# The second norm's stage of a diffusion block in written order: four output and four feed-forward tiles by token halves

## The chip, the cores and the metric

The kernel runs on one core of one Trainium2 chip. The metric is the device time of one execution in microseconds. The core's engines work side by side, each through its own queue in order: TensorE (PE, matmuls), VectorE (DVE), ScalarE (ACT), GpSimd (POOL), and SyncE (SP), which only issues transfers between HBM and on-chip memory. They wait for each other by semaphores.

## The reference, cut to what matters

One layer on 512 latent tokens of 1024 channels in float32. The change touches the passage from the mixer's output projection to the feed-forward network:

```python
x = x + g1 * (y_merged @ w_out)                       # output projection, gated residual
h2 = rmsnorm(x, norm2_g) * (1.0 + sc2) + sh2           # second norm, modulated
x = x + g2 * ((silu(h2 @ w1) * (h2 @ w3)) @ w2)        # SwiGLU, D_FF = 2816
return rmsnorm(x, final_g)

def rmsnorm(x, g):
    return x * lax.rsqrt(jnp.mean(x * x, axis=-1, keepdims=True) + EPS) * g
```

`sh1, sc1, g1, sh2, sc2, g2` come from a product of the conditioning vector with `w_ada` (adaLN).

## The kernel before, in words

Activations lie with channels on the 128 partitions and tokens along the free axis: a 1024-channel activation is 8 tiles of 128 x 512. Every float32 factor is split into a high part (rounded to fp32r) and a low remainder, and a product is three matmuls per tile of 128 channels: high weights by high input, high by low, low by high (`mm3`, lines 233 to 235; `gemm` calls it for k = 0 to 7). So one output tile of 128 channels is 24 matmuls into one PSUM bank; `psG` and `psH` hold four banks each.

Weights come as 512 KB tiles: `wsplit` takes a raw buffer `wr` (four of them, shared with the adaLN rows), loads it from SP's queue, lets ACT copy it to the high part `wh` and DVE subtract to the low part `wl` (line 215). There are four buffers of `wh` and four of `wl`; a new weight tile waits until PE has finished with the one four tiles earlier.

The second norm's stage:

- `staged_gemms("wout", ...)` does the output tiles 0 to 4 (KT - LAST = 5 of 8) over all 512 tokens. `out_tile` (lines 1459 to 1463) then adds the gated product to the residual `xr` on DVE, squares the sum on ACT and adds the square to `acc1` on DVE. The sum stays in `x1`, in the buffers named K.
- The last three output tiles go by token halves of 256 (`last_tile`): first all three for tokens 0 to 255, then for 256 to 511.
- `half_sums` sums the squares over the channels by matmuls with ones (lines 1472, 1473). `half_rms` takes mean and root (DVE, then POOL's power of -0.5, line 391) and spreads the root over the partitions with two matmuls (line 393).
- `norm2` makes the normalised input of one half, per channel tile k: `t` on DVE (line 1511: x1 times the scale am2 times the root), the high tile hTh on ACT (line 1512: t plus shift), and the low tile hTl on DVE (line 1513: t plus shift minus hTh).
- The first three feed-forward tiles (`jobs`: w1 tile 0, w3 tile 0, w1 tile 1) also go by halves; all others over 512 tokens in the loop over `f`, which calls `background()` once per f: that runs one step of `ada_later`, a load of 512 KB of w_ada into `wr` and a multiply-and-sum of 128 x 1024 on DVE (line 372) for the gate of the feed-forward network.

What sets the order: the kernel is recorded in program order and a scheduler reorders the instructions of each engine within data dependencies. `tc.high_priority` (in `wsplit`) moves instructions ahead, and `behind()` holds instructions until the matmuls of the last `gemm` are issued.

Of the kernel before, what the change touches and what calls it, by code (L numbers as in the profile page):

```python
# [1 line left out]

# [13 lines left out]
D = 1024  # L16
# [143 lines left out]
def build(nc, tc, I, out, dbg=None):  # L160
# [42 lines left out]

    def dump(name, ap):
        if dbg is not None and name in dbg:
            dma(dbg[name], ap)
# [179 lines left out]
    def rms_bcast(sums, nblk, pbank, p, tag):  # L386
        v = T(PW, [128, 8], F32, "rv", 2)
        for i, c in enumerate(sums if isinstance(sums, list) else [sums]):
            dve.tensor_scalar(v[:, i : i + c.shape[-1]], c, 1.0 / D, EPS, op0=ALU.mult, op1=ALU.add)  # L389
        r = T(PW, [128, 8], F32, "rr", 2)  # L390
        gp.tensor_tensor(r[:, :nblk], v[:, :nblk], negh[:, :nblk], op=ALU.pow)  # L391
        for b in range(nblk):
            pe.matmul(pbank[:, 128 * b : 128 * b + 128], r[:, b : b + 1].broadcast_to([128, 128]), ident, start=True, stop=True)

# [1071 lines left out]
    def half_sums(acc, sq, hf):  # L1466

        cols = []
        for b in range(2):
            sl = slice(256 * hf + 128 * b, 256 * hf + 128 * b + 128)  # L1470
            s_ = bank()[:, 0:1]
            pe.matmul(s_, acc[:, sl], ones[:, 0:1], start=True, stop=False)
            pe.matmul(s_, sq[:, sl], ones[:, 0:1], start=False, stop=True)
            cols.append(s_)
        return cols

    def half_rms(cols):
        rb = bank()
        rms_bcast(cols, 2, rb, PF, "s2")
        return rb  # L1480
# [18 lines left out]
    def last_tile(hf, d):  # L1499
        wh, wl = ws[d - KT + LAST]  # L1500
        ps = bank(psG)
        gemm(ps, wh, wl, [half(t, hf) for t in y[0]], [half(t, hf) for t in y[1]], 256)
        return out_tile(ps, 256, d, g1h, 256 * hf, xr[d], x1[d], acc1)

    def norm2(hf, cols):
        with behind():
            rb = half_rms(cols)
        for k in range(KT):
            t = scr()
            sh = modT[:, 3, k, 0:1]  # L1510
            dve.scalar_tensor_tensor(t[:, :256], half(x1[k], hf), am2[:, k : k + 1], rb[:, :256], op0=ALU.mult, op1=ALU.mult)
            act.activation(half(h2[0][k], hf), t[:, :256], AF.Identity, bias=sh)
            dve.scalar_tensor_tensor(half(h2[1][k], hf), t[:, :256], sh, half(h2[0][k], hf).bitcast(F32), op0=ALU.add, op1=ALU.subtract)

    for d in range(KT - LAST, KT):
        sq = last_tile(0, d)
    sq1 = last_tile(1, KT - LAST)
    with behind():
        cols = half_sums(acc1, sq, 0)
    sq1 = last_tile(1, KT - LAST + 1)  # L1520
    norm2(0, cols)
    for d in range(KT - LAST + 2, KT):
        sq1 = last_tile(1, d)
    ff = ([], [])
    later = ada_later(3 * KT, 4 * KT)
    lead = {}
    jobs = [("w1", 0), ("w3", 0), ("w1", 1)]
    wlead = [wsplit(I[n][f], [128, KT, 128]) for n, f in jobs]
    for hf in range(2):
        for (n, f), (wh, wl) in zip(jobs, wlead):  # L1530
            if hf == 0:
                if len(lead) == 1:
                    with behind():
                        cols = half_sums(acc1, sq1, 1)
                if len(lead) == 2:
                    norm2(1, cols)
                lead[n, f] = bank(psG)
            gemm(half(lead[n, f], hf), wh, wl, [half(t, hf) for t in h2[0]], [half(t, hf) for t in h2[1]], 256)
# [28 lines left out]
    def last_norm(hf, sq):  # L1567
        rb = half_rms(half_sums(acc2, sq, hf))
        r2 = rb[:, :256].rearrange("p (a n) -> p a n", a=1).broadcast_to([128, 2, 256])
# [40 lines left out]
```

## Time and profile before

| | us |
|---|---|
| median of 3 runs | 1218.85 (1218.58 to 1222.32) |
| profiled execution | 1219.83 |
| its span | 1218.0 |
| PE busy | 1180.8 (97%) |
| DVE busy | 833.2 (68%) |
| ACT busy | 528.9 (43%) |
| POOL busy | 87.7 (7%) |

A profile shows one execution; times count from the start of its span. A row of a timeline gives the start, the length, the engine, the line in the kernel, the operation, what it writes and reads (buffer numbers left out), the shape, how many of them, and in square brackets how long the engine had been idle and whose end it waited for. The lengths of matmuls overlap, since they are pipelined: what one costs is read from the distance of their starts. PEclk is the granted clock of TensorE, 1.00 being full.

### The profile page before, as it was taken

What the parts mean: (1) busy time and instruction counts of PE and PEld (TensorE: products, weight loads), DVE (VectorE), ACT (ScalarE), POOL (GpSimd) and SP (SyncE); (2) the same over time, 40 slices, a digit from 0 to 9 for tenths busy, and PEclk for the clock granted to TensorE, in tenths of its full rate; (3) what the DMA queues carried; (4) which work ended last, traced back from release to release, by engine and by line L of the source; (5) the groups of instructions that cost most, each with busy time, mean ns of one, the idle gap of its engine ahead of it and who ended that gap; (6) DMA issues with size and microseconds to landing.
All of it is one profiled execution on the core that took longest, in us unless ns stands there. A gap on an engine that the chain in (4) does not pass through costs nothing.

```text
span 1218.0 us, 16831 instructions
## 1 busy us (share of the span) xinstructions
PE 1180.8 (97%) x6440; PEld 1012.9 (83%) x6440; DVE 833.2 (68%) x1336; ACT 528.9 (43%) x824; POOL 87.7 (7%) x168
## 2 busy tenths in 40 slices
PE   4999999999999999999989999999999999999997
PEld 2799988888888888888778988889888888888886
DVE  5967797978989999897758896767753434432332
ACT  3754465753545444453655642333432232322221
POOL 0011110100010010101032031000000000000000
PEclk9999999999999999999989999999999999999998
DMA  9744453364244353434695686773443333233312
GB/s 346 248 159 163 136 185 106 133 237 143 75 162 137 130 174 102 147 106 155 211 319 180 196 265 218 260 234 121 140 138 104 90 100 101 85 95 96 96 48 70
DMA packets 63377, 189.04 MB, mean 155 GB/s; under 512 B 8760, under 2 KB 12608, under 8 KB 61120
## 3 DMA queue, kind: packets, MB, share of 16 engines
q1 hardware_dynamic: 51536, 150.20, 38.6%
q0 software_dynamic: 11760, 37.76, 8.7%
q8 instruction: 51, 0.84, 0.3%
q14 instruction: 30, 0.25, 0.1%
HBM read 154.37 MB, written 33.55 MB: 154 GB/s over the span
## 4 chain that ended last, share of the span: by engine, by line
PE 89%; DVE 4%; DMA 3%; ACT 2%; issue 1%; POOL 0%; SPq 0%; DVEq 0%; POOLq 0%; ACTq 0%
PE bank L233 26%; PE bank L234 26%; PE bank L235 26%; PE bank L659 2%; PE bank L660 2%; PE bank L661 2%; DMA wr<-qd 1%; DMA wr<-in_wph 1%; PE bank L616 1%; PE bank L463 1%; DVE wl L215 1%; PE bank L464 1%; ACT wh L214 1%; DMA ul<-in_xT 1%; PE bank L337 0%
## 5 line engine op out<-in xcount | busy, mean ns | idle before, releaser
L233 PE MATMUL bank<-hTh,wh 128*128 128x512 f32 (+1 forms) x952 | 366.6, 387 | 2.9 <-ACT hTh L1094 2.0
L234 PE MATMUL bank<-hTl,wh 128*128 128x512 f32 (+1 forms) x952 | 366.1, 386 | 2.9 <-DVE hTl L1100 2.2
L235 PE MATMUL bank<-hTh,wl 128*128 128x512 f32 (+1 forms) x952 | 365.6, 385 | 0.0
L214 ACT ACTIVATE wh<-wr 128x1024 fp32r<-128x1024 f32 (+1 forms) x167 | 172.2, 1033 | 400.8 <-PE bank L234 205.1
L215 DVE TENSOR_TENSOR wl<-wr,wh 128x1024 fp32r<-128x1024 f32 (+1 forms) x167 | 197.8, 1187 | 170.9 <-ACT wh L214 169.6
L233 PEld LDWEIGHTS bank<-hTh,wh 128*128 128x128 f32 x952 | 178.9, 188 | 37.5 <-ACT hTh L1094 2.2
L234 PEld LDWEIGHTS bank<-hTl,wh 128*128 128x128 f32 x952 | 179.0, 188 | 36.8 <-DVE hTl L1100 2.5
L235 PEld LDWEIGHTS bank<-hTh,wl 128*128 128x128 f32 x952 | 179.0, 188 | 34.6
L233 PE MATMUL bank<-big,wh 128*128 128x512 f32 (+1 forms) x266 | 94.7, 356 | 0.0
L234 PE MATMUL bank<-big,wh 128*128 128x512 f32 (+1 forms) x266 | 94.6, 356 | 0.0
L235 PE MATMUL bank<-big,wl 128*128 128x512 f32 (+1 forms) x266 | 94.6, 355 | 0.0
L372 DVE SCALAR_TENSOR_TENSOR wr<-wr,crow 128x1024 f32<-128x1024 f32 x32 | 38.9, 1218 | 28.3 <-DMA wr<-in_wada 28.2
L233 PEld LDWEIGHTS bank<-big,wh 128*128 128x128 f32 x266 | 50.3, 189 | 7.2
L235 PEld LDWEIGHTS bank<-big,wl 128*128 128x128 f32 x266 | 50.3, 189 | 7.1
L234 PEld LDWEIGHTS bank<-big,wh 128*128 128x128 f32 x266 | 50.3, 189 | 7.1
L214 ACT ACTIVATE hb<-hb 128x512 fp32r<-128x512 f32 (+1 forms) x49 | 36.5, 767 | 33.3 <-DVE hb L468 18.5
L1554 DVE TENSOR_TENSOR s<-s,bank 128x512 f32<-128x512 f32 x22 | 15.1, 686 | 46.4 <-PE bank L235 46.4
L391 POOL TENSOR_TENSOR rr<-rv,negh 128x2 f32<-128x2 f32 (+1 forms) x6 | 5.5, 924 | 510.7 <-DVE rv L389 510.7
L215 DVE TENSOR_TENSOR hb<-hb,hb 128x512 fp32r<-128x512 f32 (+1 forms) x49 | 40.4, 858 | 2.0 <-ACT hb L214 1.8
L659 PE MATMUL bank<-wh,hTh 128*128 128x256 f32 (+1 forms) x128 | 36.4, 285 | 0.0
L661 PE MATMUL bank<-wh,hTl 128*128 128x256 f32 (+1 forms) x128 | 36.4, 285 | 0.0
L660 PE MATMUL bank<-wl,hTh 128*128 128x256 f32 (+1 forms) x128 | 36.4, 284 | 0.0
(383 smaller groups left out, 2208.2 us busy)
## 6 DMA issues: line engine op xcount, KB each, us to landing
wr<-in_win SPq DMA_DIRECT2D x64, 512.0 KB, 3.8
wr<-in_w SPq DMA_DIRECT2D x60, 512.0 KB, 3.5
wr<-in_wada SPq DMA_DIRECT2D x32, 512.0 KB, 4.1
Kd<-K POOLq DMA_DIRECT2D x8, 1024.0 KB, 4.7
K<-Kd SPq DMA_DIRECT2D x8, 1024.0 KB, 6.4
wr<-in_wv SPq DMA_DIRECT2D x8, 512.0 KB
gmd<-s POOLq DMA_DIRECT2D x16, 256.0 KB, 2.5
wr<-in_wph SPq DMA_DIRECT2D x8, 512.0 KB, 4.2
```

The lines of the kernel that those rows point to most:

```text
L214: act.activation(hi, x, AF.Copy)
L215: dve.tensor_sub(lo, x, hi.bitcast(F32))
L233: pe.matmul(o, wh, xh, start=first, stop=False)
L234: pe.matmul(o, wh, xl, start=False, stop=False)
L235: return pe.matmul(o, wl, xh, start=False, stop=last)
L372: dve.scalar_tensor_tensor(w, w, 1.0, crow[:], op0=ALU.mult, op1=ALU.mult, accum_out=s)
L463: pe.matmul(ps[:], lhs, w4h, start=True, stop=False)
L464: pe.matmul(ps[:], lhs, w4l, start=False, stop=True)
L659: pe.matmul(o, xh, wh, start=bool(k == 0), stop=False)
L660: pe.matmul(o, xh, wl, start=False, stop=False)
L661: m = pe.matmul(o, xl, wh, start=False, stop=bool(k == KT - 1))
L1554: dve.tensor_tensor(t[:], t[:], pb[:], op=ALU.mult)
```

## The change

Four output tiles (LAST = 4) and four feed-forward tiles (w3 tile 1 is added) go by token halves. The stage is recorded by hand in the intended order, and a new context, `in_order`, chains the instructions of each engine inside it, so that the scheduler keeps that order on every engine. In the feed-forward tiles, `high_first` issues for one tile first the eight products of high weights and high inputs, then the eight of low weights and high inputs, then the eight of high weights and low inputs. The residual of the last four output tiles is loaded into buffers of the "big" pool, and at output tile 0 two steps of `ada_later` run in place of one. `rms_bcast` is cut into `rms_columns` (mean and root) and `rms_spread` (the two matmuls), so that other work can stand between them. The lines of the changed file are 14 to 24 higher: DVE's t is L1535, hTl L1537, ACT's hTh L1536, the adaLN row L386, wl L229.

```diff
+    @contextmanager
+    def in_order():
+        traced = nc.cur_bb.bb.instructions
+        n, last = len(traced), {}
+        yield
+        for i in traced[n:]:
+            if i.engine in last:
+                tc.add_manual_dep(
+                    i, last[i.engine], mybir.DependencyInfo(mybir.DependencyClass.NoSync, mybir.DependencyReason.DATA), reason="in_order"
+                )
+            last[i.engine] = i.name
...
-    LAST = 3
+    LAST = 4
     for d in range(KT):
-        xr.append(scr())
+        xr.append(scr() if d < KT - LAST else big(F32))
...
         out_tile(ps, SEQ, d, g1h, 0, xr[d], x1[d], acc1)
-        background()
+        steps(2 if d == 0 else 1)
...
-    def norm2(hf, cols):
-        with behind():
-            rb = half_rms(cols)
-        for k in range(KT):
+    def norm2(hf, r, ks):
+        for k in ks:
             t = scr()
             sh = modT[:, 3, k, 0:1]
-            dve.scalar_tensor_tensor(t[:, :256], half(x1[k], hf), am2[:, k : k + 1], rb[:, :256], op0=ALU.mult, op1=ALU.mult)
+            dve.scalar_tensor_tensor(t[:, :256], half(x1[k], hf), am2[:, k : k + 1], r, op0=ALU.mult, op1=ALU.mult)
             act.activation(half(h2[0][k], hf), t[:, :256], AF.Identity, bias=sh)
             dve.scalar_tensor_tensor(half(h2[1][k], hf), t[:, :256], sh, half(h2[0][k], hf).bitcast(F32), op0=ALU.add, op1=ALU.subtract)
...
+    def high_first(j, hf, between=None):
+        ps, (wh, wl), n = half(lead[jobs[j]], hf), wlead[j], 0
+        for w, x in ((wh, 0), (wl, 0), (wh, 1)):
+            if x and between:
+                between()
+            for k in range(KT):
+                n += 1
+                pe.matmul(ps, w[:, k], half(h2[x][k], hf), start=n == 1, stop=n == 3 * KT)
+
+    def lead_weights(j):
+        n, f = jobs[j]
+        wlead.append(wsplit(I[n][f], [128, KT, 128]))
+        lead[n, f] = bank(psG)
...
+    jobs = [("w1", 0), ("w3", 0), ("w1", 1), ("w3", 1)]
+    d0 = KT - LAST
+    with in_order():
+        for d in range(d0, KT):
+            last_tile(0, d)
+            sq = last_out(0, d)
+        last_tile(1, d0, range(4))
+        r = half_sums(acc1, sq, 0)
+        last_tile(1, d0, range(4, KT))
+        last_out(1, d0)
+        last_tile(1, d0 + 1, range(2))
+        r0 = half_rms(r)
+        norm2(0, r0, (0, 1))
+        last_tile(1, d0 + 1, range(2, KT))
+        lead_weights(0)
+        norm2(0, r0, (2, 3))
+        last_out(1, d0 + 1)
+        last_tile(1, d0 + 2)
+        norm2(0, r0, (4, 5))
+        last_out(1, d0 + 2)
+        lead_weights(1)
+        last_tile(1, d0 + 3)
+        norm2(0, r0, (6, 7))
+        sq1 = last_out(1, d0 + 3)
+        high_first(0, 0, lambda: spread.append(half_sums(acc1, sq1, 1)))
+        lead_weights(2)
+        high_first(1, 0, lambda: spread.append(half_rms(spread[0])))
+        r1 = spread[1]
+        norm2(1, r1, (0, 1, 2))
+        lead_weights(3)
+        high_first(2, 0)
+        norm2(1, r1, (3, 4, 5))
+        high_first(3, 0)
+        norm2(1, r1, (6, 7))
+        for j in range(4):
+            high_first(j, 1)
```

Three places in the queues as built show what moves. PE's order is the same in both kernels up to output tile 4, and again from the first tile after w3,1 on. In the rows, K is x1, bank the PSUM tile, and s2 a scratch tile (t, or a square).

First place: DVE in the first half's norm. Before, the rows of k = 4 to 6 (those of k = 1 to 3 stand likewise, with a weight split between):

```order
L1511 SCALAR_TENSOR_TENSOR s2_1461_8299<-K_1379_7885,am2_1296_7486,bank_1454_8275 128x256
L1511 SCALAR_TENSOR_TENSOR s2_1462_8303<-K_1379_7885,am2_1296_7486,bank_1454_8275 128x256
L1511 SCALAR_TENSOR_TENSOR s2_1463_8307<-K_1379_7885,am2_1296_7486,bank_1454_8275 128x256
L1513 SCALAR_TENSOR_TENSOR hTl_1438_8121<-s2_1461_8299,modT_6_78,hTh_1430_8113 128x256
L1513 SCALAR_TENSOR_TENSOR hTl_1439_8122<-s2_1462_8303,modT_6_78,hTh_1431_8114 128x256
L1513 SCALAR_TENSOR_TENSOR hTl_1440_8123<-s2_1463_8307,modT_6_78,hTh_1432_8115 128x256
```

Three t (L1511) come ahead of the three low tiles that need ACT's result. The same place on DVE after, from k = 3 to k = 5, with an output tile's operations and the adaLN row (wr and crow) between:

```order
L1535 SCALAR_TENSOR_TENSOR s2_1463_8298<-K_1378_7884,am2_1296_7486,bank_1455_8258 128x256
L1537 SCALAR_TENSOR_TENSOR hTl_1435_8091<-s2_1463_8298,modT_6_78,hTh_1427_8083 128x256
L1481 SCALAR_TENSOR_TENSOR K_1379_7885<-bank_1454_8251,g1h_1294_7484,big_1386_7897 128x256
L386 SCALAR_TENSOR_TENSOR wr_1500_8645,modT_6_78<-wr_1500_8645,crow_918_5517 128x1024
L1485 TENSOR_TENSOR s2_1380_7886<-s2_1380_7886,s2_1464_8303 128x256
L1535 SCALAR_TENSOR_TENSOR s2_1466_8331<-K_1379_7885,am2_1296_7486,bank_1455_8258 128x256
L1537 SCALAR_TENSOR_TENSOR hTl_1436_8092<-s2_1466_8331,modT_6_78,hTh_1428_8084 128x256
L1535 SCALAR_TENSOR_TENSOR s2_1467_8335<-K_1379_7885,am2_1296_7486,bank_1455_8258 128x256
L1537 SCALAR_TENSOR_TENSOR hTl_1437_8093<-s2_1467_8335,modT_6_78,hTh_1429_8085 128x256
L1481 SCALAR_TENSOR_TENSOR K_1379_7885<-bank_1465_8306,g1h_1294_7484,big_1387_7899 128x256
L386 SCALAR_TENSOR_TENSOR wr_1503_8654,modT_6_78<-wr_1503_8654,crow_918_5517 128x1024
```

Now t and hTl alternate through all eight k, and two adaLN rows stand between them.

Second place: SP's queue behind the last residual load. Before (lines 254 and 362 issue weights and adaLN rows):

```order
L254 DMA wr_1467_8343<-in_w1 128x1024
L254 DMA wr_1470_8349<-in_w3 128x1024
L254 DMA wr_1473_8355<-in_w1 128x1024
L362 DMA wr_1494_8561<-in_wada 128x1024
L254 DMA wr_1495_8563<-in_w3 128x1024
L362 DMA wr_1501_8601<-in_wada 128x1024
L254 DMA wr_1502_8604<-in_w1 128x1024
```

The adaLN rows stand behind three feed-forward weight tiles and between the next. SP's queue after:

```order
L268 DMA wr_1458_8287<-in_w1 128x1024
L268 DMA wr_1469_8343<-in_w3 128x1024
L268 DMA wr_1481_8421<-in_w1 128x1024
L268 DMA wr_1489_8467<-in_w3 128x1024
L376 DMA wr_1500_8645<-in_wada 128x1024
L376 DMA wr_1503_8654<-in_wada 128x1024
L268 DMA wr_1504_8657<-in_w1 128x1024
```

All four lead weight tiles are loaded first; the two adaLN rows after them use the buffer of the first one, wr_1458, one after the other.

Third place: PE at the start of the feed-forward tiles. Before, it takes products of the first k for all three tiles as they become ready:

```order
L233 MATMUL bank_1476_8361<-hTh_1426_8109,wh_1468_8344 128x256
L234 MATMUL bank_1476_8361<-hTl_1434_8117,wh_1468_8344 128x256
L235 MATMUL bank_1476_8361<-hTh_1426_8109,wl_1469_8345 128x256
L233 MATMUL bank_1479_8392<-hTh_1426_8109,wh_1471_8350 128x256
L234 MATMUL bank_1479_8392<-hTl_1434_8117,wh_1471_8350 128x256
L235 MATMUL bank_1479_8392<-hTh_1426_8109,wl_1472_8351 128x256
```

The first k's high and low tiles serve six matmuls of two banks. After, PE goes through the eight high tiles for one bank:

```order
L1547 MATMUL bank_1461_8293<-hTh_1424_8080,wh_1459_8288 128x256
L1547 MATMUL bank_1461_8293<-hTh_1425_8081,wh_1459_8288 128x256
L1547 MATMUL bank_1461_8293<-hTh_1426_8082,wh_1459_8288 128x256
L1547 MATMUL bank_1461_8293<-hTh_1427_8083,wh_1459_8288 128x256
L1547 MATMUL bank_1461_8293<-hTh_1428_8084,wh_1459_8288 128x256
L1547 MATMUL bank_1461_8293<-hTh_1429_8085,wh_1459_8288 128x256
L1547 MATMUL bank_1461_8293<-hTh_1430_8086,wh_1459_8288 128x256
L1547 MATMUL bank_1461_8293<-hTh_1431_8087,wh_1459_8288 128x256
L1547 MATMUL bank_1461_8293<-hTh_1424_8080,wl_1460_8289 128x256
```

The eighth matmul needs the high tile of k = 7, and no other tile's work stands ahead of it.

More of the change, by code (lines that the diff above doesn't have):

```diff
@@ L1 @@
 import math
+from contextlib import contextmanager
 import numpy as np
@@ L1474, in half_sums, with half_rms @@
             cols.append(s_)
[L1475 to L1477 removed]
+        return rms_columns(cols)
+    def half_rms(r):
         rb = bank()
[L1479 to L1480 removed]
+        rms_spread(r, 2, rb)
+        return rb[:, :256]
     xq = [T(PT, [128, 4, SEQ], F32, "K") for _ in range(2)]
@@ L1497, in build, with last_tile @@
     h2 = ([slots("hTh")() for _ in range(KT)], [slots("hTl")() for _ in range(KT)])
-    def last_tile(hf, d):
+    def last_tile(hf, d, ks=range(KT)):
         wh, wl = ws[d - KT + LAST]
-        ps = bank(psG)
-        gemm(ps, wh, wl, [half(t, hf) for t in y[0]], [half(t, hf) for t in y[1]], 256)
-        return out_tile(ps, 256, d, g1h, 256 * hf, xr[d], x1[d], acc1)
-    def norm2(hf, cols):
-        with behind():
-            rb = half_rms(cols)
-        for k in range(KT):
+        if ks[0] == 0:
+            tile_ps[d] = bank(psG)
+        gemm(tile_ps[d], wh, wl, [half(t, hf) for t in y[0]], [half(t, hf) for t in y[1]], 256, ks)
@@ L1524, in build @@
+    def lead_weights(j):
+        n, f = jobs[j]
+        wlead.append(wsplit(I[n][f], [128, KT, 128]))
+        lead[n, f] = bank(psG)
     ff = ([], [])
     later = ada_later(3 * KT, 4 * KT)
[L1526 to L1538, printed above, removed]
+    lead, wlead, tile_ps, spread = {}, [], {}, []
```

28 lines of the change are left out of this document (13 added, 15 removed).

## The prediction

> **What bounds the kernel now.** I read the page first, for the engine that ends last.
>
> ```profile
> span 1218.0 us, 16831 instructions
> PE 1180.8 (97%) x6440; PEld 1012.9 (83%) x6440; DVE 833.2 (68%) x1336; ACT 528.9 (43%) x824; POOL 87.7 (7%) x168
> PE 89%; DVE 4%; DMA 3%; ACT 2%; issue 1%; POOL 0%; SPq 0%; DVEq 0%; POOLq 0%; ACTq 0%
> ```
>
> TensorE (PE) is busy for 97% of the span and carries 89% of the chain of waits: every microsecond in which PE stands still is a microsecond of the kernel. Then I took the stage in the table of windows, from the first matmul of output tile 4, up to which PE's order is the same in both kernels, to the first matmul behind the feed-forward tile w3,1, from which it is the same again.
>
> ```profile
> 816.04:867.19 51.15, 49.19 (x361) 46.41 (x360) 38.09 (x72) 21.48 (x38) 2.44 (x2) 1.00 0.35 108
> ```
>
> The columns are the stretch, its length, and the busy times of PE, weight load, DVE, ACT and POOL, then granted clock, DMA share and GB/s. PE idles 1.96 us in 51.15, and DVE is already busy for 38. The timeline of PE shows where:
>
> ```profile
> 841.66 0.62 PE L233 MATMUL bank<-hTh,wh 128*128 128x256 f32 x3 [0.35 <-ACT hTh L1512]
> 842.92 0.39 PE L234 MATMUL bank<-hTl,wh 128*128 128x256 f32 x1 [0.64 <-DVE hTl L1513]
> 851.11 0.71 PE L393 MATMUL bank<-mats,rr 128*128 128x128 f32 x4 [0.45 <-POOL rr L391]
> 852.93 0.86 PE L233 MATMUL bank<-hTh,wh 128*128 128x256 f32 x4 [0.53 <-ACT hTh L1512]
> ```
>
> Four short waits for the normalised tiles and the root: that is all that a better order can win here.
>
> **The change part by part: PE's own work.** Starts of matmuls in PE's timeline give the price of each form:
>
> ```profile
> 816.04 0.39 PE L233 MATMUL bank<-big,wh 128*128 128x512 f32 x1
> 821.48 0.28 PE L233 MATMUL bank<-big,wh 128*128 128x256 f32 x1
> 832.99 0.28 PE L1472 MATMUL bank<-mats,s 128*128 128x1 f32 x2
> 834.00 0.28 PE L234 MATMUL bank<-big,wh 128*128 128x256 f32 x1
> 836.76 0.60 PE L393 MATMUL bank<-mats,rr 128*128 128x128 f32 x4
> 837.32 0.28 PE L234 MATMUL bank<-big,wh 128*128 128x256 f32 x1
> 867.19 0.39 PE L233 MATMUL bank<-hTh,wh 128*128 128x512 f32 x1
> ```
>
> 24 matmuls of 512 columns take 821.48 - 816.04 = 5.44 us; the 96 of 256 that follow take 11.51, so 0.1199 each and 2.88 for a half tile. The sums of squares cost 834.00 - 832.99 - 0.12 = 0.89, the spread of the root 837.32 - 836.76 - 0.12 = 0.44. Two tiles go from one of 512 to two halves: 2 x (5.76 - 5.44) = **+0.63 us**. Without waits the stage before would take 2 x 5.44 + 12 x 2.88 + 2 x (0.89 + 0.44) = 48.07 us; it took 51.15. So the waits with their slow restarts are worth 3.08, which **-3.08** takes away if all of them go. After: 16 x 2.88 + 2.66 = 48.7 without waits.
>
> Reordering the three products by high and low moves no work; it needs the eight high tiles earlier, within 8 x 0.12 = 0.96 us, and the low ones later. So the last high tile, hTh of k = 7, sets when PE goes on.
>
> **The normalisation in written order.** Per k, DVE multiplies (t), ACT adds the shift (hTh), DVE subtracts (hTl). Before, DVE ran three t, then three hTl. Now the order on DVE is t, hTl, t, hTl: hTl waits for ACT, and the next t stands behind it.
>
> ```profile
> L1511 DVE SCALAR_TENSOR_TENSOR s<-K,am,bank x16: 469/472/480, 837.4 to 857.0; 128x256 f32<-128x256 f32 x16
> L1512 ACT ACTIVATE hTh<-s,modT x16: 491/495/510, 838.1 to 857.5; 128x256 fp32r<-128x256 f32 x16
> 851.86 1.26 DVE L1511 SCALAR_TENSOR_TENSOR s<-K,am,bank 128x256 f32<-128x256 f32 x3 [1.58 <-PE bank L393]
> 852.37 1.31 ACT L1512 ACTIVATE hTh<-s,modT 128x256 fp32r<-128x256 f32 x3 [5.07 <-DVE s L1511]
> 857.10 0.91 ACT L1512 ACTIVATE hTh<-s,modT 128x256 fp32r<-128x256 f32 x2 [1.05 <-DVE s L1511]
> 857.64 0.88 DVE L1513 SCALAR_TENSOR_TENSOR hTl<-s,modT,hTh 128x256 fp32r<-128x256 f32 x2 [0.19 <-ACT hTh L1512]
> ```
>
> From start of t to start of hTh 852.37 - 851.86 = 0.51; hTh takes 0.495; hTl starts 857.64 - 857.10 - 0.495 = 0.045 behind its end; DVE takes one more 256-column operation per (1.26 - 0.47) / 2 = 0.39. One k is thus 0.51 + 0.495 + 0.045 + 0.39 = 1.44 us, against 0.79 of DVE's work. Eight take 7 x 1.44 + 1.00 = 11.1 us to the last hTh.
>
> Between them on the same queue stand the weight splits (ACT wh, then DVE wl) and two rows of the adaLN product (L386, a 128x1024 operation on a freshly loaded wr):
>
> ```profile
> 840.15 1.06 ACT L214 ACTIVATE wh<-wr 128x1024 fp32r<-128x1024 f32 x1 [1.55 <-PE bank L234]
> 841.24 1.22 DVE L215 TENSOR_TENSOR wl<-wr,wh 128x1024 fp32r<-128x1024 f32 x1 [0.18 <-ACT wh L214]
> 842.39 1.27 DVE L1513 SCALAR_TENSOR_TENSOR hTl<-s,modT,hTh 128x256 fp32r<-128x256 f32 x3
> wr<-in_wada SPq DMA_DIRECT2D x32, 512.0 KB, 4.1
> wr<-in_wada SPq DMA_DIRECT2D x6, 512.0 KB, 4.5
> 818.41 0.33 SPq L362 DMA_DIRECT2D wr<-in_wada  x1
> 821.93 1.22 DVE L372 SCALAR_TENSOR_TENSOR wr<-wr,crow 128x1024 f32<-128x1024 f32 x1 [0.16 <-DMA wr<-in_wada]
> ```
>
> A 128x1024 operation holds DVE for 842.39 - 841.24 = 1.15. Both adaLN loads use the slot that lead weight 0 leaves, one after the other on SP's queue: the first is issued once its wl is done, the second once the first product is done. A load takes 4.1 (all), 4.5 (this stretch) or 3.5 us (818.41 to 821.93); I take 4.1, in the middle. First half, added to the 11.1: wl of lead 0 waits for its wh behind hTh of k = 1, 0.58 idle + 1.15 = 1.73; then an output tile 0.39, 0.84 left of the load (4.1 less 3.27 of work), the product 1.14, an addition 0.39 = 2.76; then 0.39, 0.44 left of the second load, 1.14, 0.39 and wl of lead 1 1.14 = 3.5. Together **19.1 us**.
>
> Its start: the addition for output tile 4, second half.
>
> ```profile
> 827.43 0.48 DVE L1459 SCALAR_TENSOR_TENSOR K<-bank,g1h,s 128x256 f32<-128x256 f32 x1 [0.49 <-PE bank L235]
> 828.01 0.42 ACT L1461 ACTIVATE s<-K 128x256 f32<-128x256 f32 x1 [2.02 <-DVE K L1459]
> 832.87 0.28 PE L235 MATMUL bank<-big,wl 128*128 128x256 f32 x1
> 833.19 0.48 DVE L1459 SCALAR_TENSOR_TENSOR K<-bank,g1h,s 128x256 f32<-128x256 f32 x1 [2.40 <-PE bank L235]
> 834.23 1.74 POOL L391 TENSOR_TENSOR rr<-rv,negh 128x2 f32<-128x2 f32 x1 [79.46 <-DVE rv L389]
> ```
>
> On the clock of this profile the four first halves end at 816.04 + 4 x 2.88 = 827.55, tile 4's second half with the sums at 831.32; 0.20 + 0.58 + 0.42 behind that its squares are there, and with the addition t of k = 0 starts at 832.95. The spread (832.04, read 851.86 - 851.11 = 0.75 later) is no later. POOL's root is done 834.23 + 1.74 - 832.99 = 2.98 behind the start of the sums and now has 0.89 + 18 x 0.12 = 3.05: just hidden; without that, some tenths. The last hTh of the half stands at 832.95 + 19.1 = 852.05, while PE would want it at 832.48 + 18 x 0.12 + 2 x 2.88 + 0.84 = 841.23: **+10.8 us**. The squares of the last output tile, behind hTl of k = 7 on DVE, add **+0.2** at the second sums.
>
> Second half: the low-weight products (0.96), the sums (0.89), the eight low ones (0.96) and 16 products of lead 1 (1.92) bring the spread to 857.1, t of k = 0 to 857.8. Chain 11.1 + 0.7 (an adaLN product, in part under ACT's time) + 1.73 (wl of lead 3) = 13.5, so the last hTh at 871.3. PE, with 8 + 48 + 8 products after the spread, would want it at 865.1: **+6.2 us**, part of it shown as a wait for wh of lead 3. Afterwards 88 products of 0.12 run free to 881.9.
>
> xT into "big" tiles, two adaLN steps at tile 0, and the loads of wout moved on SP's queue I cost at nothing: the DVE and SP rows ahead of the stage hold the same operations, and of PE's waits in this stage none lies ahead of 841.66. Were that cover gone, one late wout load would cost up to 4.1.
>
> **The clock.** Where PE stood longer, its clock fell:
>
> ```profile
> 32.61 0.80 PE L234 MATMUL bank<-hTl,wh 128*128 128x512 f32 x1 [2.22 <-DVE hTl L1100]
> 35.34 0.50 PE L234 MATMUL bank<-hTl,wh 128*128 128x512 f32 x1
> 630.40 0.76 PE L233 MATMUL bank<-uh,K 128*128 128x512 f32 x1 [3.35 <-DVE dx L943]
> 635.23 0.63 PE L235 MATMUL bank<-uh,K 128*128 128x512 f32 x1
> 34.00:36.00 2.00, 2.00 (x7) 1.58 (x6) 1.97 (x3) 1.96 (x4) 0.00 (x0) 0.61 1.05 385
> 632.00:633.00 1.00, 1.00 (x4) 0.81 (x3) 1.00 (x3) 0.00 (x0) 0.93 (x2) 0.50 1.11 373
> 840.40:855.00 14.60, 12.64 (x99) 11.71 (x98) 11.21 (x27) 5.75 (x13) 0.70 (x1) 1.00 0.32 104
> ```
>
> After 32.61 seven matmuls took 0.43 in place of 0.227 (35.34 is the last): 1.4 us lost. After 630.40, some thirteen: 2.7. In 840.40:855.00, with waits below 1 us, nothing was lost. The first chain gives waits of some 3.4 and 4.9 us with one matmul between; I take one fall, **+2.0**, the middle of 1.4 and 2.7. The second chain's waits are 1.3 to 2.1 long, nearer to the last row: nothing; its bound is 2.7 again.
>
> The Trainium skill, page "TensorE: Matmul & The Clock Gate", Part 1, says that the array runs at half clock after an idle window of about 3.4 us and comes back after a busy window of that length. By that rule, this change's waits would cost 1.7 us per fall (an estimate from that page), and the sum would be 0.3 lower; the traced 0.50 agrees, and the 5.8 us to recover after 630.40 is longer than it says.
>
> **Sum.** 0.63 - 3.08 + 10.8 + 0.2 + 6.2 + 2.0 = +16.75 us. The profiled execution took 1219.83 (span 1218.0 and 1.8 around it), 0.98 above the median 1218.85: 1236.6, and against the median 1235.6.
>
> **Rivals.** (a) The clock falls in the second chain too: 2.05 more, 1237.6; for it speaks that five high products are spread over 5 us there. (b) It never falls: 1233.6; against it are the two falls above. (c) DVE's rate, not its waiting, decides: rows between t 0 and hTh 7 hold 11.97 us of DVE work and the second half 8.7; waits 4.2 and 1.4, so 0.63 - 3.08 + 5.6 = +3.2, 1222.0. For it: DVE overlaps neighbours in the groups of three. Against: hTl cannot start before its own hTh. (d) The other side, not slower: the written order hides both chains behind PE, and only 0.63 - 3.08 = -2.45 stays, 1216.4. It decides at 841.23 - 832.95 = 8.3 us for the first chain, which is under DVE's bare work. A gain above 3.08 isn't there to be had. (e) The order doesn't come about as written: the queues as built show that it does; what stays open is only a load of wout that is late, in the range.
>
> **How the numbers follow.** The forecast 0.56, (a) 0.18, (b) 0.15, (c) 0.05, (d) 0.03, a late load or something else 0.03. Bounds: load 3.5 or 4.5 is -0.9 or +1.0, 0.03 in the step of 1.44 is 0.5 over 16, clock 0 to 5.4 in place of 2.0: 1231.2 to 1240.5, widened to 1230 to 1241. About 0.3% (3.7 us) is what a measurement here can tell from no change: faster 0.01, same 0.07 ((c) and (d)), slower 0.92.
>
> **What would show it.** After: PE waits for ACT hTh in the lead tiles, some 10 us in the first half and 5 in the second; starts of t 1.44 apart on DVE; the stage from tile 4 to the tile behind w3,1 about 68 us for 51.15; a clock near 0.5 to 0.8 for some us after the first chain. Wrong, if t starts every 0.8 us, if PE reaches the spread of the second half before 850, or if waits stand ahead of tile 4.

## The result, and the profile after

The change makes the kernel slower: 1239.88 us (median of 4 runs, 1238.46 to 1240.2) against 1218.9 of the kernel before beside it, a ratio of 1.0167 with a 95% interval of 1.0154 to 1.018. The prediction was 1235.6 with a range of 1230 to 1241. The profiled execution took 1239.71 us.

The head of the page and its row of engines:

```profile
span 1237.8 us, 16932 instructions
PE 1188.8 (96%) x6488; PEld 1021.3 (83%) x6488; DVE 834.8 (67%) x1338; ACT 530.0 (43%) x825; POOL 87.8 (7%) x168
```

PE counts 8.0 us more as busy (1188.8 for 1180.8), though two half tiles in place of whole ones add only 0.63: matmuls at half clock are busy for longer (in PE's timeline below, 0.58 in place of 0.38 for a single one). The stage itself, from the first matmul of output tile 4 to the first behind w3,1, in the table of windows (columns as before: length, PE, weight load, DVE, ACT, POOL, clock):

```profile
816.44:887.54 71.10, 57.41 (x409) 55.52 (x408) 38.56 (x72) 21.55 (x36) 2.35 (x2) 0.86 0.24 75
```

71.10 us for 51.15: 19.95 more, and the span is 19.8 longer. The whole difference between these two executions lies in this stage. DVE's work is nearly the same (38.56 for 38.09); PE stands still for 13.7 us of it, and its mean clock is 0.86. PE's timeline, with L1547 the products of `high_first` and L412 the spread of the root:

```profile
840.79 0.64 PE L1547 MATMUL bank<-hTh,wh 128*128 128x256 f32 x4
844.13 0.38 PE L1547 MATMUL bank<-hTh,wh 128*128 128x256 f32 x1 [2.70 <-ACT hTh L1536]
845.59 0.38 PE L1547 MATMUL bank<-hTh,wh 128*128 128x256 f32 x1 [1.07 <-ACT hTh L1536]
850.15 0.58 PE L1547 MATMUL bank<-hTh,wh 128*128 128x256 f32 x1 [4.18 <-ACT hTh L1536]
851.60 0.58 PE L1547 MATMUL bank<-hTh,wh 128*128 128x256 f32 x1 [0.87 <-ACT hTh L1536]
860.12 0.61 PE L412 MATMUL bank<-mats,rr 128*128 128x128 f32 x4
866.18 1.22 PE L1547 MATMUL bank<-hTh,wh 128*128 128x256 f32 x8 [1.62 <-ACT wh L228]
871.28 0.38 PE L1547 MATMUL bank<-hTh,wh 128*128 128x256 f32 x1 [1.07 <-ACT hTh L1536]
874.19 0.58 PE L1547 MATMUL bank<-hTh,wh 128*128 128x256 f32 x1 [1.06 <-ACT hTh L1536]
887.54 0.40 PE L247 MATMUL bank<-hTh,wh 128*128 128x512 f32 x1
```

Four high products run at once (k = 0 to 3), then each waits for its own hTh. The eighth starts at 851.60 instead of 840.79 + 7 x 0.12 = 841.63: 9.97 us. In the second half it starts at 874.19; 0.36 for the spread and 63 products of 0.12 behind 860.12 would be 868.03: about 6.2. What DVE does meanwhile:

```profile
833.29 0.47 DVE L1535 SCALAR_TENSOR_TENSOR s<-K,am,bank 128x256 f32<-128x256 f32 x1
834.34 0.48 DVE L1537 SCALAR_TENSOR_TENSOR hTl<-s,modT,hTh 128x256 fp32r<-128x256 f32 x1 [0.58 <-ACT hTh L1536]
834.74 0.47 DVE L1535 SCALAR_TENSOR_TENSOR s<-K,am,bank 128x256 f32<-128x256 f32 x1
841.57 1.23 DVE L386 SCALAR_TENSOR_TENSOR wr<-wr,crow 128x1024 f32<-128x1024 f32 x1 [0.30 <-DMA wr<-in_wada]
846.36 1.22 DVE L386 SCALAR_TENSOR_TENSOR wr<-wr,crow 128x1024 f32<-128x1024 f32 x1
850.53 0.47 DVE L1535 SCALAR_TENSOR_TENSOR s<-K,am,bank 128x256 f32<-128x256 f32 x1
```

The first two t's (L1535) start 1.45 us apart, with 0.58 idle ahead of the low tile (L1537); of the two adaLN rows (L386) the first waits 0.30 for its load and the second not at all. The clock in the table of windows (the number ahead of the last two):

```profile
840.00:846.00 6.00, 2.19 (x14) 1.60 (x13) 4.16 (x10) 1.79 (x4) 0.00 (x0) 1.00 0.41 134
846.00:858.00 12.00, 6.98 (x31) 6.69 (x32) 6.77 (x14) 3.74 (x6) 1.63 (x1) 0.50 0.33 93
858.00:860.00 2.00, 2.00 (x12) 2.00 (x12) 0.00 (x0) 0.00 (x0) 0.00 (x0) 0.60 0.59 231
872.00:874.00 2.00, 0.39 (x1) 0.19 (x1) 1.02 (x3) 0.88 (x2) 0.00 (x0) 0.81 0.00 0
874.00:880.00 6.00, 5.81 (x27) 5.82 (x28) 1.18 (x2) 1.68 (x3) 0.00 (x0) 0.50 0.00 0
880.00:884.00 4.00, 4.00 (x35) 4.00 (x35) 2.75 (x4) 1.58 (x2) 0.00 (x0) 0.99 0.44 133
```

It fell twice, once in each half, and came back only 8.0 and 5.9 us after PE had gone on without waits.

### The profile page after: what moved, and what is told of

It is laid out like the page before. It is cut to its first block, busy times and chain, and to the rows that moved or that the text cites. A ratio compares the mean times of both kernels' runs of the same rounds, so it can differ in the third digit from the quotient of the medians.

```text
span 1237.8 us, 16932 instructions
## 1 busy us (share of the span) xinstructions
PE 1188.8 (96%) x6488; PEld 1021.3 (83%) x6488; DVE 834.8 (67%) x1338; ACT 530.0 (43%) x825; POOL 87.8 (7%) x168
## 4 chain that ended last, share of the span: by engine, by line
PE 56%; issue 29%; DMA 5%; DVE 4%; POOL 2%; ACT 2%; SPq 0%; POOLq 0%; DVEq 0%; ACTq 0%
PE bank L247 15%; PE bank L248 15%; PE bank L249 15%; PE bank L681 2%; PE bank L682 2%; PE bank L683 2%; PE bank L1547 2%; DMA wr<-in_wph 1%; DVE wl L229 1%; DMA mats<-in_mats 1%; DMA hb<-in_dftf 1%; DMA wr<-kd 1%; ACT wh L228 1%; DMA wr<-qd 1%; DMA K<-in_wada 0%
## 5 line engine op out<-in xcount | busy, mean ns | idle before, releaser
L247 PE MATMUL bank<-hTh,wh 128*128 128x512 f32 x896 | 351.5, 393 | 1.9 <-ACT hTh L1116 1.9
L248 PE MATMUL bank<-hTl,wh 128*128 128x512 f32 x896 | 350.4, 391 | 1.9 <-DVE hTl L1122 1.9
L249 PE MATMUL bank<-hTh,wl 128*128 128x512 f32 x896 | 350.0, 391 | 0.0
L229 DVE TENSOR_TENSOR wl<-wr,wh 128x1024 fp32r<-128x1024 f32 (+1 forms) x167 | 198.0, 1188 | 174.4 <-ACT wh L228 173.1
L247 PEld LDWEIGHTS bank<-hTh,wh 128*128 128x128 f32 x896 | 168.9, 189 | 35.7 <-ACT hTh L1116 2.1
L248 PEld LDWEIGHTS bank<-hTl,wh 128*128 128x128 f32 x896 | 168.8, 188 | 35.5 <-DVE hTl L1122 2.4
L249 PEld LDWEIGHTS bank<-hTh,wl 128*128 128x128 f32 x896 | 168.7, 188 | 34.7
L247 PE MATMUL bank<-big,wh 128*128 128x512 f32 (+1 forms) x274 | 96.1, 351 | 0.0
L248 PE MATMUL bank<-big,wh 128*128 128x512 f32 (+1 forms) x274 | 96.1, 351 | 0.0
L386 DVE SCALAR_TENSOR_TENSOR wr<-wr,crow 128x1024 f32<-128x1024 f32 x32 | 38.9, 1219 | 28.1 <-DMA wr<-in_wada 28.1
L248 PEld LDWEIGHTS bank<-big,wh 128*128 128x128 f32 x274 | 51.8, 189 | 6.9
L247 PEld LDWEIGHTS bank<-big,wh 128*128 128x128 f32 x274 | 51.8, 189 | 6.8
L229 DVE TENSOR_TENSOR hb<-hb,hb 128x512 fp32r<-128x512 f32 (+1 forms) x49 | 40.5, 860 | 2.0 <-ACT hb L228 2.0
```

Source lines behind the costliest of these rows:

```text
L229: dve.tensor_sub(lo, x, hi.bitcast(F32))
L247: pe.matmul(o, wh, xh, start=first, stop=False)
L248: pe.matmul(o, wh, xl, start=False, stop=False)
L249: return pe.matmul(o, wl, xh, start=False, stop=last)
L386: dve.scalar_tensor_tensor(w, w, 1.0, crow[:], op0=ALU.mult, op1=ALU.mult, accum_out=s)
```

## The experiments

All kernels are the changed one with an edit, except e6 and e8, which edit the kernel before. Ratios are to the kernel before, timed beside each on the same chip (1218.7 to 1218.95 us). The stage's length is that of the profiled execution, between the two matmuls named above (in e8 the scheduler mixes whole and half tiles, so that it can't be cut there).

| kernel | median us | ratio and interval | stage us |
|---|---|---|---|
| before | 1218.9 | | 51.15 |
| the change | 1239.88 | 1.0167 (1.0154 to 1.018) | 71.10 |
| e1_groups | 1228.73 | 1.0087 (1.0067 to 1.0107) | 58.87 |
| e2_ada_later | 1237.41 | 1.0153 (1.0138 to 1.0168) | 68.89 |
| e3_groups_ada_later | 1226.46 | 1.0063 (1.0045 to 1.0081) | 57.83 |
| e4_fill | 1232.82 | 1.0120 (1.0104 to 1.0137) | 64.90 |
| e5_scheduler_order | 1219.9 | 1.0008 (0.9998 to 1.0019) | 50.79 |
| e6_sizes_alone | 1218.39 | 0.9995 (0.9982 to 1.0007) | 49.40 |
| e7_all_t_first | 1218.73 | 0.9991 (0.9981 to 1.0001) | 48.73 |
| e8_alternation_alone | 1229.21 | 1.0078 (1.0064 to 1.0092) | |
| e9_fill_first_half | 1235.28 | 1.0131 (1.0109 to 1.0153) | 67.78 |
| e10_fill_second_half | 1238.29 | 1.0164 (1.0146 to 1.0183) | 69.31 |
| e11_groups_ada_fill | 1223.52 | 1.0045 (1.0030 to 1.0060) | 54.32 |
| e12_product_order | 1236.26 | 1.0145 (1.0124 to 1.0165) | 67.05 |

**e1_groups: t's of a piece behind one another.** The pieces of two or three channel tiles stay where the change put them, but inside each piece DVE does all t's, then all low tiles.

```diff
-        for k in ks:
-            t = scr()
-            dve.scalar_tensor_tensor(t[:, :256], half(x1[k], hf), am2[:, k : k + 1], r, ...)
-            act.activation(half(h2[0][k], hf), t[:, :256], AF.Identity, bias=sh)
-            dve.scalar_tensor_tensor(half(h2[1][k], hf), t[:, :256], sh, ...)
+        ts = [scr() for _ in ks]
+        for t, k in zip(ts, ks):
+            dve.scalar_tensor_tensor(t[:, :256], half(x1[k], hf), am2[:, k : k + 1], r, ...)
+        for t, k in zip(ts, ks):
+            act.activation(half(h2[0][k], hf), t[:, :256], AF.Identity, bias=...)
+        for t, k in zip(ts, ks):
+            dve.scalar_tensor_tensor(half(h2[1][k], hf), t[:, :256], ...)
```

> Within each piece of the norm (two or three channel tiles) DVE now makes all t, then ACT all hTh, then DVE all hTl; everything else as in the changed kernel. Theory (hTl and the next t take turns on DVE, 1.44 us per tile): the step falls to about 0.9 in pairs and 0.8 in threes, 4 us less in the first half and 5 in the second, so waits of about 6 and 1 us in place of 10 and 6, and if no wait passes 3 us the clock stays up, 6 us more: 1225 to 1231. Rival (the two additional split tiles and the product order cost the time): within 2 us of 1239.9.

Measured 1228.73, 11.2 us below the change. One long wait is left in PE's timeline, and the clock fell only there:

```profile
846.99 0.98 PE L1548 MATMUL bank<-hTh,wh 128*128 128x256 f32 x2 [5.05 <-ACT hTh L1536]
864.15 0.79 PE L1548 MATMUL bank<-hTh,wh 128*128 128x256 f32 x2 [0.41 <-ACT hTh L1536]
```

In the second half the delay of 6.2 us shrinks to a wait of 0.4. More than half of the loss, with one of the two falls of the clock in it, hangs on the order of two kinds of operation on one queue.

**e2_ada_later: the two adaLN rows behind the stage.** Each `background()` of the first f's is held, engine by engine, behind the stage's last instruction.

```diff
-        background()
+        if f < 4:
+            with past_stage():
+                background()
+        else:
+            background()
```

> The adaLN rows are held behind the last norm operation of the stage on DVE and SP; the alternation stays. Theory (alternation first, adaLN rows a smaller part of the first chain: 0.3 + 1.14 + 1.14 us, and 0.7 in the second): 2 to 3.3 us less, the clock still falls twice: 1236.5 to 1238. Rival (the loads and products of adaLN, which stand among the norm's operations, are the main cause): 10 us less or more, below 1230.

Measured 1237.41, inside the forecast; the stage is 2.21 us shorter. The first half's chain on DVE shows how little the rows had cost there (timeline of DVE, L1495 the output tile, L1499 the addition of its squares, L243 the weight split):

```profile
831.66 0.47 DVE L1549 SCALAR_TENSOR_TENSOR s<-K,am,bank 128x256 f32<-128x256 f32 x1
840.19 0.42 DVE L1499 TENSOR_TENSOR s<-s,s 128x256 f32<-128x256 f32 x1 [0.54 <-ACT s L1497]
845.41 1.23 DVE L243 TENSOR_TENSOR wl<-wr,wh 128x1024 fp32r<-128x1024 f32 x1 [0.52 <-ACT wh L242]
848.01 0.47 DVE L1549 SCALAR_TENSOR_TENSOR s<-K,am,bank 128x256 f32<-128x256 f32 x1
```

From the first t to the last it takes 16.35 us here and 850.53 - 833.29 = 17.24 in the change: 0.89 less for two rows of 1.15. Without them DVE stands idle for the squares and for wh, on which ACT had been at work under the rows' cover. The forecast was met in part by luck: of the 2.21 us, 1.11 come from the end of the stage, from the second half's eighth high product on (883.70 - 871.46 = 12.24, in the change 887.54 - 874.19 = 13.35). The work and the waits there are the same, but the clock came back after 3.41 us in this execution and after 6.83 in the change's (the last section says more on this).

**e3_groups_ada_later: both edits.**

> Both of the last two edits. Theory: first wait 3 to 4 us, second under 1, hardly any loss by the clock: 1221 to 1225, still not below the kernel before, since 0.63 us of split tiles and a first wait remain. Rival (clock falls in any case): 1227 to 1229.

Measured 1226.46, above the forecast and 0.5 below the rival, whose fall of the clock came. PE has one wait left in the stage, and the clock is 0.50 in the 8 us behind it (timeline of PE, then windows):

```profile
843.69 0.98 PE L1562 MATMUL bank<-hTh,wh 128*128 128x256 f32 x2 [4.18 <-ACT hTh L1550]
```

```profile
844.00:848.00 4.00, 4.00 (x19) 3.91 (x19) 1.20 (x6) 1.40 (x3) 0.00 (x0) 0.50 0.31 117
848.00:852.00 4.00, 4.00 (x20) 4.00 (x21) 1.22 (x2) 0.00 (x0) 1.62 (x1) 0.50 0.38 124
```

I had expected no fall any more. The wait comes from the pieces' places: t of k = 6 stands behind an output tile, an addition and a weight split.

**e4_fill, e9_fill_first_half, e10_fill_second_half: the clock by itself.** DVE's order stays; PE gets dummy matmuls, whose results nobody reads, into a spare bank in its waits: 82 of them, or the 61 of the first half, or the 21 of the second.

```diff
+    FILL = ({3: 18, 4: 7, 5: 30, 6: 6}, {4: 7, 5: 7, 6: 7})   # e9: ({...}, {}); e10: ({}, {...})
                 pe.matmul(ps, w[:, k], half(h2[x][k], hf), start=n == 1, stop=n == 3 * KT)
+                if j == 0 and n <= KT:
+                    for _ in range(FILL[hf].get(k, 0)):
+                        pe.matmul(spare[:, :256], w[:, 0], half(h2[0][0], hf), start=True, stop=True)
```

> The changed kernel, with 82 matmuls of 256 columns into a spare bank where PE waits for high tiles (18, 7, 30 and 6 in the first half, 7, 7 and 7 in the second), so that PE is busy while it waits; they add nothing to the output. Theory (two falls of the clock cost 6 us of the 21): the clock stays at 1.0 through the stage and the time falls by 4 to 6 us, 1234 to 1236. Rival (the time is lost in the waits alone, the clock row is only a sign of them): 1239 to 1241, or longer by the part of the fill that doesn't fit.

> The changed kernel with dummy matmuls (their results go to a spare bank) in TensorE's waits of the first half alone (61 of the 82 of e4_fill). Theory: the two clock falls are separate, each caused by the waits just ahead of it; the fall at 846 us cost 3.4 us, the one at 873 us stays at about 2.5 us: 1236 to 1237 us. Rival (the second fall needs the first, the clock gives way more easily after a stretch at half speed): both go, 1233 or less.

> The changed kernel with dummy matmuls in the three waits of the second half alone (21 of the 82). Theory: 2.4 to 2.6 us less, 1237 to 1238 us; the fall at 846 us stays. Rival: the first fall holds most of the loss that e4_fill gave back: 1239 or more.

e4_fill measured 1232.82, 7.1 below the change and 1.2 below the forecast; its stage is 6.20 shorter, at a clock of 1.00 throughout:

```profile
814.70:879.60 64.90, 60.96 (x491) 59.08 (x490) 38.35 (x72) 21.68 (x36) 2.34 (x2) 1.00 0.26 83
```

```profile
849.69 0.39 PE L1550 MATMUL bank<-hTh,wh 128*128 128x256 f32 x1 [0.36 <-ACT hTh L1536]
854.76 0.60 PE L412 MATMUL bank<-mats,rr 128*128 128x128 f32 x4
868.82 0.39 PE L1550 MATMUL bank<-hTh,wh 128*128 128x256 f32 x1 [0.23 <-ACT hTh L1536]
879.60 0.40 PE L247 MATMUL bank<-hTh,wh 128*128 128x512 f32 x1
```

The windows row holds 82 matmuls more, and less time. From the eighth high product to the spread the same work takes 854.76 - 849.69 = 5.07 us here, 860.12 - 851.60 = 8.52 in the change: the first fall cost 3.45. From the second half's eighth high product to the end it takes 10.78 here and 887.54 - 874.19 = 13.35 there: 2.57. e9 (1235.28, 4.6 below; stage 3.32 shorter) keeps the second fall and e10 (1238.29, 1.6 below; stage 1.79 shorter) the first; so the two are separate, and each is made by the waits just ahead of it. Both came out some tenths outside the forecast, in opposite directions. For e10 its trace says why: its own first fall took 861.45 - 852.53 = 8.92 up to the spread, 0.40 more than the change's, and reached past it (0.93 us for the spread's row, 0.61 in the change), since its clock was at 0.50 for 17.07 us in place of 13.65:

```profile
852.53 0.58 PE L1550 MATMUL bank<-hTh,wh 128*128 128x256 f32 x1 [0.87 <-ACT hTh L1536]
861.45 0.93 PE L412 MATMUL bank<-mats,rr 128*128 128x128 f32 x4
```

For e9 the stage agrees with the forecast (3.32 for 3.4); its runs lie between 1233.41 and 1237.28. e4's 7.1 is likewise 0.9 more than its stage explains.

**e11_groups_ada_fill: e3 with its one wait filled.**

```diff
+                if (j, hf, n) == (0, 0, 6):
+                    for _ in range(33):
+                        pe.matmul(spare[:, :256], w[:, 0], half(h2[0][0], hf), start=True, stop=True)
```

> e3_groups_ada_later with 33 dummy matmuls in its one wait of 4.2 us, behind the sixth high product of feed-forward tile 0. Theory: what kept it 7.7 us above the kernel before is that wait and the clock's fall behind it; without the fall 3 to 4 us go: 1222.5 to 1223.5 us. Rival: e3's remainder is not the clock but the written order of the rest: 1225.5 or more.

Measured 1223.52; the stage 54.32 for 57.83:

```profile
814.92:869.24 54.32, 54.05 (x443) 53.02 (x441) 36.01 (x69) 20.59 (x36) 2.35 (x2) 1.00 0.29 93
```

So 3.51 us of e3's remainder was the clock. What is left above the 48.7 without waits is 5.6: the filled wait itself (33 x 0.12 and 0.2 of waiting) and 1.4 that I did not follow further.

**e5_scheduler_order: the change without the written order.** The edges of `in_order` are left out; sizes, pieces and products stay.

```diff
         for i in traced[n:]:
-            if i.engine in last:
-                tc.add_manual_dep(i, last[i.engine], ...)
             last[i.engine] = i.name
```

> The changed kernel with the edges of the written order left out: four tiles of each kind by halves, highs first and split squares stay, but the scheduler places the instructions inside each engine. Theory: the written order's alternation of t and hTl on DVE (with what stands between them) is what costs, not the sizes and not the products' order; the scheduler puts three t's behind one another, as in the kernel before, and the stage loses under 2 us: 1217 to 1222 us. Rival: highs first itself leaves TensorE too little to do while hTh tiles come, and the low products stand in the way whatever DVE does: 1228 or more.

Measured 1219.9, inside the forecast: within 0.2% of the kernel before, and 20 us below the change. PE waits twice in the stage (0.7 and 0.3 us). DVE does run the t's mostly in threes and twos; its row behind the second spread and the window of the stage:

```profile
850.35 1.26 DVE L1531 SCALAR_TENSOR_TENSOR s<-K,am,bank 128x256 f32<-128x256 f32 x3 [1.35 <-PE bank L408]
```

```profile
816.63:867.42 50.79, 49.66 (x410) 49.02 (x409) 36.40 (x71) 20.54 (x36) 2.33 (x2) 1.00 0.34 105
```

**e6_sizes_alone: the kernel before with four tiles of each kind by halves.**

```diff
-    LAST = 3
+    LAST = 4
-        xr.append(scr())
+        xr.append(scr() if d < KT - LAST else big(F32))
-        background()
+        steps(2 if d == 0 else 1)
-    jobs = [("w1", 0), ("w3", 0), ("w1", 1)]
+    jobs = [("w1", 0), ("w3", 0), ("w1", 1), ("w3", 1)]
```

The edit also takes over the change's "big" buffers for the residual and its two adaLN steps at output tile 0, so it tests those as well.

> The kernel before with four output tiles and four feed-forward tiles by halves (three before), nothing else: products interleaved, the scheduler's order. The prediction priced the two extra split tiles at 0.63 us: 1219 to 1220.5 us, with waits as in the kernel before. Rival: the fourth tile ties up a buffer of wh or a bank, so that a weight tile comes late: 1222 or more.

Measured 1218.39, no difference that shows, and 0.6 below the forecast. The stage is 1.75 us shorter than before, not 0.63 longer, since the waits all but vanish: PE is busy for 49.27 us of 49.40. That this comes from the fourth half tile between the root and its use is my reading; no run tests it.

```profile
818.28:867.68 49.40, 49.27 (x410) 48.86 (x409) 35.12 (x69) 20.45 (x36) 2.44 (x2) 1.00 0.33 103
```

**e7_all_t_first: a written order that works.** Behind each spread come all eight t's, into buffers of their own, and the eight hTh on ACT; low tiles, weight splits, sums and adaLN rows later.

```diff
+    def highs(hf, r):
+        for k in range(KT):
+            ts[k] = big(F32)
+            dve.scalar_tensor_tensor(ts[k][:, :256], half(x1[k], hf), am2[:, k : k + 1], r, ...)
+        for k in range(KT):
+            act.activation(half(h2[0][k], hf), ts[k][:, :256], AF.Identity, bias=...)
...
         r0 = half_rms(r)
-        norm2(0, r0, (0, 1))
+        highs(0, r0)
         last_tile(1, d0 + 1, range(2, KT))
```

> A written order that keeps DVE's queue clear: behind each spread all eight t's of the half (in buffers of their own), the eight hTh right behind on ACT, the low tiles and the weights' low parts later, the second sums at the end of feed-forward tile 0 and the spread at the end of tile 1, adaLN rows behind the stage. Theory (no wait for hTh, no clock fall; what stays are +0.63 for the split tiles and -3.08 for the waits of before): 1216 to 1218.5 us, a little below the kernel before. Rival: written order costs something of its own wherever DVE is full for 8 us at a stretch, and a wait for wl or the sums comes up with a clock fall behind it: 1221 to 1225.

The stage (windows), and DVE's timeline at the first spread:

```profile
814.62:863.35 48.73, 48.73 (x410) 48.72 (x408) 34.85 (x69) 19.94 (x36) 2.33 (x2) 1.00 0.32 98
```

```profile
831.47 3.22 DVE L1551 SCALAR_TENSOR_TENSOR big<-K,am,bank 128x256 f32<-128x256 f32 x8
835.00 1.66 DVE L1559 SCALAR_TENSOR_TENSOR hTl<-big,modT,hTh 128x256 fp32r<-128x256 f32 x4
```

PE works for all 48.73 us of the stage, which is the prediction's 48.7 without waits. Eight t's take 3.22 us, and all hTh are there before PE asks. The written order is thus no fault in itself (this one also has the adaLN rows behind the stage). The median of 1218.73, 0.2 above the forecast, doesn't show the 2.4 us, though: executions differ ahead of the stage, whose start lies between 814.03 (e3) and 818.28 (e6) in these profiles, and the interval of the ratio reaches from 0.9981 to 1.0001. Whether something ahead of the stage gives the gain back is not settled.

**e8_alternation_alone: the kernel before with t and hTl alternating.**

```diff
             m = dve.scalar_tensor_tensor(t[:, :256], half(x1[k], hf), ...)
+            if k:
+                tc.add_manual_dep(m.ins, lows[-1].name, ...)
```

> The kernel before with one thing changed: each t of the second norm is held on DVE behind the low tile of the channel tile before it, so that t and hTl alternate; sizes, products and all else as before. Theory: eight steps of 1.45 us per half in place of about 0.9 make the last low tile of each half some 4 us later, and the interleaved products can cover only part: 4 to 9 us slower, 1223 to 1228, with the clock falling at most once. Rival (the cost needs the late recording of the pieces and highs first as well): under 1221.

Measured 1229.21, 10.3 slower and 1.2 above the forecast's end. The second half's chain in DVE's timeline:

```profile
855.68 0.48 DVE L1513 SCALAR_TENSOR_TENSOR s<-K,am,bank 128x256 f32<-128x256 f32 x1 [1.58 <-PE bank L393]
856.74 0.48 DVE L1519 SCALAR_TENSOR_TENSOR hTl<-s,modT,hTh 128x256 fp32r<-128x256 f32 x1 [0.58 <-ACT hTh L1518]
866.91 0.48 DVE L1519 SCALAR_TENSOR_TENSOR hTl<-s,modT,hTh 128x256 fp32r<-128x256 f32 x1 [0.58 <-ACT hTh L1518]
870.70 4.63 DVE L215 TENSOR_TENSOR wl<-wr,wh 128x1024 fp32r<-128x1024 f32 x4 [3.31 <-ACT wh L214]
```

```profile
876.08 0.47 PE L233 MATMUL bank<-hTh,wh 128*128 128x512 f32 x1 [3.39 <-DVE s L1560]
```

From the first t to the end of the last low tile it takes 867.39 - 855.68 = 11.7 us, where the kernel before needed 857.64 + 0.88 - 851.86 = 6.7. Its scheduler covers most of that by putting w3 tile 1 between, so PE waits only 3.0 us in the halves (2.0 in the kernel before); but no buffer of wh comes free in that time, four weight splits come at once (4.63 us), and PE stands 3.39 us behind the stage, for the feed-forward product that waits behind them on DVE. The clock fell twice, not at most once: it was 0.50 from 857.08 to 860.49, in the second half, and from 877.56 to 880.97, soon after the long wait. So the alternation costs by itself, but I had the place wrong.

**e12_product_order: the three products of a channel tile together, in the change.**

```diff
-        for w, x in ((wh, 0), (wl, 0), (wh, 1)):
-            if x and between:
-                between()
-            for k in range(KT):
+        for k in range(KT):
+            for w, x in ((wh, 0), (wh, 1), (wl, 0)):
                 n += 1
                 pe.matmul(ps, w[:, k], half(h2[x][k], hf), ...)
+        if between:
+            between()
```

> The changed kernel with the three products of each channel tile together (high by high, high by low, low by high), as the kernel before has them, the second sums behind the last product of feed-forward tile 0 and the spread behind the last of tile 1; order and sizes as in the changed kernel. Theory: behind the last hTh of a half the changed kernel has 17 products of its tile left, here 3, against 0.5 us for the last hTl: 1.2 us less per half, 1236 to 1238.5 us. Rival: highs first makes no difference or helps, since the low products fill no wait: 1239 to 1241.

Measured 1236.26, 3.6 below the change, at the forecast's lower end. With late tiles, highs first is thus the worse order here. The reason that I gave, 17 products left behind the last hTh for 3 here, is shown only in part: from the first product of feed-forward tile 0 to the spread the traces differ by 0.80 us (18.53 here, 19.33 in the change), from the spread to the end by 3.26 (24.16 for 27.42). In the second half PE no longer waits for hTh at all; it waits 2.58 for wh and 0.74 for wl of lead 3, and the clock falls there instead. In e5 and e7, where the tiles are early, highs first costs nothing.

## Why the prediction was right, and what it mis-sized

Forecast +16.75 us in the stage, measured +19.95; as times 1235.6 and 1239.88, inside the range but near its upper end. The waits for hTh in both halves were forecast rightly, the number of the clock's falls and their price were not. By the prediction's own steps:

- **PE's own work, +0.63, and the waits of before, -3.08.** Right: e7's stage takes 48.73 for 48.7.
- **The alternation, 1.44 us per channel tile.** Right: 1.45 measured, with 0.58 idle for ACT in each. e1 shows that it causes more than half of the loss: grouped, 11.2 us go. The rest hangs on where the pieces stand in the written order: e3 keeps a wait of 4.18 us, e7 has none, and the scheduler's placing loses nothing (e5).
- **First half, +10.8.** 9.97. The start of the first t (832.95 forecast, 833.29 less the 0.40 by which this execution started later) was met; the loads of the adaLN rows took 3.5 us, the lower of the two bounds, so the rows waited 0.30 for the 1.28 forecast.
- **Second sums, +0.2.** Not there: PE doesn't wait at the sums, at half clock in the change or at full clock in e4.
- **Second half, +6.2.** 6.2, with the wait for wh of lead 3 (1.62) in it, as said.
- **The clock, +2.0 for one fall.** This step failed: two falls, 3.45 + 2.57 = 6.0 us, shown by e4, e9 and e10. The first was mis-sized: I took the middle of falls that had cost 1.4 and 2.7, and this one cost 3.45: the clock stayed at 0.50 for the 8 us from 851.60 to about 859.6. The second, which I costed at nothing because its waits are shorter than 2.1 us and gave to rival (a), came in full, behind waits of 1.07 each. Together they lie above the 5.4 that I had as the upper bound. In the total, the 4.0 us too few for the clock are partly offset by 1.0 us too many for the first half and the sums; the median lies 1.1 us inside the range's upper end.
- **The bounds.** Summed again from their own terms they are 1232.1 to 1240.3, not 1231.2 to 1240.5: the lower end has 1 us too much taken off, and loads of 3.5 and 4.5 us give -1.0 and +0.8.

The measured terms give 0.63 - 3.08 + 9.97 + 6.2 + 6.0 = 19.7 of the 19.95. Rival (a), with two falls, named the right mechanism but kept the low price (1237.6). Rivals (b), (c) and (d) are out: the clock fell, and DVE's bare rate isn't the bound, since nearly the same DVE work in another order (36.40 us in e5, for 38.56) costs nothing. The buffers and adaLN steps costed at nothing cost nothing that shows (e6).

## What to carry to other kernels

When a two-engine chain (DVE, ACT, DVE) is written out by hand, put all of the first step ahead of the last step on the queue that holds both; alternating them turned 0.8 us of work into a step of 1.45 here. If the tensor engine must wait for such tiles, try the product order that leaves least to do after the last one (it gained 3.6 us here), and price a fall of its clock for each chain of waits apart from the waits themselves. A scheduler that already groups is worth testing with the new sizes alone before an order is fixed by hand.

## What the runs showed of the hardware

A granted clock of 0.50 came with waits of only 1.07 us each, three in a row with one matmul between (the second half). In the first half it fell 4.7 us behind the last four products that ran together, in the second 3.2 us behind the last five. After the last wait it came back 8.0 us later in the first half and 5.9 in the second. Windows of 0.1 us place the four changes, since the clock of a row is a mean:

```profile
845.90:846.00 0.10, 0.07 (x1) 0.00 (x0) 0.10 (x2) 0.00 (x0) 0.00 (x0) 0.74 0.02 0
859.60:859.70 0.10, 0.10 (x3) 0.10 (x2) 0.00 (x0) 0.00 (x0) 0.00 (x0) 0.99 0.53 205
873.20:873.30 0.10, 0.00 (x0) 0.00 (x0) 0.10 (x2) 0.00 (x0) 0.00 (x0) 0.78 0.00 0
880.00:880.10 0.10, 0.10 (x2) 0.10 (x2) 0.10 (x1) 0.00 (x0) 0.00 (x0) 0.59 0.00 0
```

They lie at 845.95, 859.60, 873.26 and 880.08: 13.65, 13.65 and 6.83 us apart, which are 4, 4 and 2 steps of 3.413. The other traces with falls in the stage or just behind it agree: the clock stayed at 0.50 for one step in e2's second fall and both of e8's, two in e9's and e12's second, three in e1 and e3, four in the first of e2 and e12, and five in e10. The two falls of the kernel before that the prediction priced at 1.4 and 2.7 us had lasted one step (32.14 to 35.56) and two (629.48 to 636.31). Where the steps lie against the work differs between executions, so the same waits can cost different amounts: the second half's fall 2.57 us in the change and 12.24 - 10.78 = 1.46 in e2, the first half's 3.45 in the change and 3.85 in e10 up to the spread alone. One trace of a fall is therefore a poor price for the next.

The Trainium skill, page "TensorE: Matmul & The Clock Gate", Part 1 (The HAM clock gate), gives an idle window of about 3.4 us for the fall and a busy window of the same length for the return. The traced step of 3.41 us agrees with that length. The lone matmuls between the waits did not keep the clock up, and the 8.0 and 5.9 us from the last wait to the return are longer than one window. Filling the waits with 82 matmuls that compute nothing kept it at 1.00 and made the kernel 7.1 us faster, 6.20 of them in the stage.
